# The first token half turned ahead at the end of a stage, in a two-layer transformer on one core

## The chip, the cores and the metric

The kernel runs on one core of one Trainium2 chip. The core has a matrix engine (PE), a vector engine (DVE), a scalar engine (ACT), GpSimd (POOL) and SyncE (SP), which only issues DMAs here, and 16 DMA engines that bring data from device memory into the on-chip memory. PE writes its results into banks of a separate accumulator memory (PSUM), from which DVE and ACT read them. Each engine has its own list of instructions and waits for the others by semaphores. The metric is the device time of one execution in microseconds (us).

## The reference

256 tokens of width 1024 go through seven parts, each of which adds its result to the residual `h`, with an RMS norm ahead of it. Cut to what matters:

```python
h = x
h = h + even_mixer(rms_norm(h, ln_mix[0]), ...)        # layer0_mix
h = h + swiglu(rms_norm(h, ln_ffn[0]), ...)            # f0, width 2816
h = h + gated_deltanet(rms_norm(h, ln_mix[1]), ...)    # gdn
h = h + moe_swiglu(rms_norm(h, ln_ffn[1]), ...)        # 8 experts, 2 per token, width 3584
...
def rmsnorm(x, w):
    xf = x.astype(jnp.float32)
    y = xf * lax.rsqrt(jnp.mean(xf * xf, axis=-1, keepdims=True) + EPS)
    return (y * w.astype(jnp.float32)).astype(x.dtype)
...
def swiglu_2(x, w_gu, w_down):
    g, u = jnp.split(x @ w_gu, 2, axis=-1)
    return (jax.nn.silu(g) * u) @ w_down
```

The second block follows on the same tokens: a feed-forward part (f1, width 2816), a token mixing with three branches (mixing) and another feed-forward part (f2, width 2816). Its parts have a second norm behind them (`f1post`, `mixpost`, `f2post`), ahead of the sum with the residual. Everything is fp32.

## The kernel before

**Precision and weights.** Each fp32 operand is split into a high part and the rest, and a product is three matmuls: high x high, high x low of either side (`mm3`, L274). The weights come as units of 1 MB. `Stream._load` (L204) issues a unit's DMA into a `raw` buffer, `_piece` (L221) lets ACT copy its half into `hi` (L229) and DVE subtract to `lo` (L230). There are two `raw` buffers for the whole program, and a feed-forward stage adds six of its own from the stage's memory pool. That memory was the stage's before, so the first DMA into one of them waits until the last reader of what lay there is done.

**Tokens.** The 256 tokens are two halves, t = 0 and t = 1, of 128 rows: `h[t]`. At the end of a stage each half gets its sum, and at four places `norm(t)` (L438) follows at once: ACT squares both 512-wide parts with a row sum, DVE forms `rs`, POOL raises it to -0.5, DVE writes `xn` (L269) in two instructions. After f1 and mixing `post_add` (L1253) stands ahead of it, the second norm with the same pattern (`pj`, `prs`). The next stage begins with `norm_T` (L425). It calls `norm_turn(0)` (L454), which lets PE transpose the half in two groups of four 128x128 blocks (L280), each into a PSUM bank; then ACT copies a bank into the high part of `x` and DVE subtracts to its low part (L292). The turn of the second half is kept as `turn_late` and called some way into the stage.

**The feed-forward stages.** `ffn` (L567) goes over 11 blocks f of 256 columns. For each and each half, 24 matmuls of gate and up go into a bank `gu`; ACT and DVE make `hv` from it; PE transposes it (`tr`), it is split into `hh` and `hl`, and 12 matmuls add to the two banks `y`. At the last block `done(t)` is called as soon as the half's `y` is complete. layer0_mix and mixing end with `out_proj`, whose matmuls write banks `mm`.

**What sets the order.** The code says which operation needs which; when the program is built, a list scheduler places the operations in one list per engine, with its own estimate of their times. On the chip each engine takes its list in order. Names in a row are those of tiles: `gu<-hi,x` is a gate and up matmul with weights `hi` that writes bank `gu`. In layer0_mix and the experts the banks of `norm_turn` are called `gu` before, in gdn and mixing `sd`, after the function that the next stage hands in.

Of the kernel before, what the change touches and what calls it, by code (L numbers as in the profile page):

```python
# [181 lines left out]
class Stream:  # L182
    def __init__(self, nc, rawp, hip, units, ends):
        self.nc, self.hip, self.units, self.ends = nc, hip, units, list(ends)
        self.pools = {0: [rawp, NRAW, []], 1: [None, 0, []]}
        self.raw, self.hi, self.lo = {}, {}, {}
        self.i = self.nl = self.np = 0
        self.limit = self.stop = 0
# [58 lines left out]
class Kernel:  # L247
    def __init__(self, ctx, tc, a, out):
        self.ctx, self.tc, self.nc, self.a, self.out = ctx, tc, tc.nc, a, out
        self.sides = []  # L250
        self.nev = 0
        self.moe_es = None
        self.normed = {}


    def act(self, out, in_, func, **kw):
# [167 lines left out]
    def norm_T(self, ps, late=False):  # L424

        for t in range(2):
            if t not in self.normed:
                self.norm(t)
        self.norm_turn(0, ps)
        self.turn_late = lambda: self.norm_turn(1, ps)  # L430
        if not late:
            self.turn_late()
        if self.gains:
            self.rowload(self.gain, self.gains.pop(0))
        self.W.open()

    def norm(self, t):

        h = self.h[t]
        ss = self.st.tile([128, 2], F32, name="ss", tag="ss")  # L440
        rs = self.st.tile([128, 1], F32, name="rs", tag="rs")
        xn = self.xn("xn")
        for n in range(2):
            s = slice(n * 512, n * 512 + 512)
            self.act(xn[:, s], h[:, s], AF.Square, scale=1.0 / 32, accum_out=ss[:, n:n + 1])
        self.ts(rs, ss[:, 0:1], ss[:, 1:2], EPS, ADD, ADD)
        self.last_pow = self.nc.gpsimd.tensor_tensor(rs, rs, self.mhalf[:, 0:1], ALU.pow)  # L447
        for n in range(2):
            s = slice(n * 512, n * 512 + 512)
            self.last_xn = self.stt(xn[:, s], h[:, s], rs, self.gain[:, s], MUL, MUL)  # L450
        self.normed[t] = xn

    def norm_turn(self, t, ps):
        xn, tok = self.normed.pop(t), slice(t * 128, t * 128 + 128)  # L454
        for n in range(2):
            p = ps()
            for c in range(4):
                self.tr(p[:, c * 128:c * 128 + 128], xn[:, n * 512 + c * 128:n * 512 + c * 128 + 128])
            self.split(self.xh[:, 4 * n:4 * n + 4, tok], self.xl[:, 4 * n:4 * n + 4, tok],
                       p.rearrange("p (c t) -> p c t", c=4))  # L460
# [193 lines left out]
    def layer0_mix(self):  # L654
        nc, tc, W = self.nc, self.tc, self.W
        with ExitStack() as es:
            pool = es.enter_context(tc.tile_pool(name="l0", bufs=1))
            sd, ps = self.banks("sd", "a"), self.banks("mm", "b")
# [208 lines left out]
            def add(t, n, p):  # L867
                s = slice(n * 512, n * 512 + 512)
                self.tt(self.h[t][:, s], p, self.h[t][:, s], ADD)
                if n == 1 and self.gains:  # L870
                    self.norm(t)
            self.drive(self.out_proj((yh, yl), ps, add))


# [353 lines left out]
    def ffn_phase(self, name, nf, post=None, final=False):  # L1228
        nc, tc = self.nc, self.tc
        with ExitStack() as es:  # L1230
            pool = es.enter_context(tc.tile_pool(name=name, bufs=1))
            gu, tr, y4 = self.banks("gu", "a"), self.banks("tr", "a"), self.banks("y", "b")
            self.W.phase(pool, 6)
            self.pad(pool, 128)
            self.norm_T(gu, True)
            with self.after(self.last_pow):
                pw = None if post is None else self.rowload(pool.tile([128, 1024], F32, name="pw"), post)
            y = [[y4(), y4()] for _ in range(2)]

            def done(key, t, yt):  # L1240
                if pw is None:
                    for n in range(2):
                        s = slice(n * 512, n * 512 + 512)
                        self.tt(self.h[t][:, s], yt[n], self.h[t][:, s], ADD)
                else:
                    self.post_add(t, yt, pw, 0.5, final)
                if not final:
                    self.norm(t)
            seq = [((self.xh, self.xl), 0, f == 0, f == nf - 1) for f in range(nf)]
            self.drive(self.ffn(seq, 2, pool, gu, tr, lambda key: y, done, first=self.turn_late))  # L1250

# [24 lines left out]
    def moe(self):  # L1276
# [4 lines left out]
        with ExitStack() as es:  # L1281
# [123 lines left out]
            def scatter(e, yh, yl):  # L1405
                for t in range(2):
                    for n in range(2):
                        s = slice(n * 512, n * 512 + 512)
                        p = sc()
                        self.mm(p, ohT[e][:, t * 128:t * 128 + 128], yh[:, s], True, False)  # L1410
                        self.mm(p, ohT[e][:, t * 128:t * 128 + 128], yl[:, s], False, True)
                        self.stt(self.h[t][:, s], p, gate[:, t, e:e + 1], self.h[t][:, s], MUL, ADD)
                        yield
                    if e == 7 and self.gains:
                        self.norm(t)

            def done(e, t, yt):
                yh, yl = (self.xn(n, dt=F32R) for n in ("yh", "yl"))
                for n in range(2):
                    s = slice(n * 512, n * 512 + 512)  # L1420
                    self.split(yh[:, s], yl[:, s], yt[n])
                self.sides.append(scatter(e, yh, yl))
# [81 lines left out]
    def mixing(self):  # L1504
        nc, tc, W = self.nc, self.tc, self.W
        with ExitStack() as es:
            pool = es.enter_context(tc.tile_pool(name="mx", bufs=1))
            sd, ps = self.banks("sd", "a"), self.banks("mm", "b")
# [330 lines left out]
            def fin(t, n, p):  # L1839
                z[t].append(p)  # L1840
                if n == 1:
                    self.post_add(t, z[t], pw, 1.0)
                    self.norm(t)
            self.drive(self.out_proj(X, ps, fin, True))


# [81 lines left out]
```

## Time and profile before

| what | before |
| --- | --- |
| median of 3 runs | 2270.36 us (2268.29 to 2271.34) |
| profiled execution | 2270.24 us, span 2268.5 us |
| PE busy | 2203.4 us, 97% of the span |
| DVE busy | 1709.2 us, 75% |
| ACT busy | 1390.6 us, 61% |
| POOL busy | 194.6 us, 9% |
| moved by DMA | 561.65 MB, 248 GB/s on average |

A span is the time from the first to the last instruction of one profiled execution; the 1.7 us by which its own time is longer lie around it. The busy shares are means over seven stages. What an edit at a stage's end is worth is read from the rows of that place.

### The profile page before, as it was taken

What the parts mean: (1) busy time and instruction counts of PE and PEld (TensorE: products, weight loads), DVE (VectorE), ACT (ScalarE), POOL (GpSimd) and SP (SyncE); (2) the same over time, 40 slices, a digit from 0 to 9 for tenths busy, and PEclk for the clock granted to TensorE, in tenths of its full rate; (3) what the DMA queues carried; (4) which work ended last, traced back from release to release, by engine and by line L of the source; (5) the groups of instructions that cost most, each with busy time, mean ns of one, the idle gap of its engine ahead of it and who ended that gap; (6) DMA issues with size and microseconds to landing.
All of it is one profiled execution on the core that took longest, in us unless ns stands there. A gap on an engine that the chain in (4) does not pass through costs nothing.

```text
span 2268.5 us, 29759 instructions
## 1 busy us (share of the span) xinstructions
PE 2203.4 (97%) x11398; PEld 1818.9 (80%) x11398; DVE 1709.2 (75%) x2220; ACT 1390.6 (61%) x1978; POOL 194.6 (9%) x324
## 2 busy tenths in 40 slices
PE   7899999998998999999999999999999999999998
PEld 6788877886887888888888888887887888787886
DVE  7754558876997999999999999995546667676544
ACT  5844456545776777777777777774445446345442
POOL 2000003232000000000100000000000000000000
PEclk9999999999999999999999999999999999999999
DMA  7375433225997999989999999977533543456540
GB/s 266 128 293 182 149 108 112 76 96 230 365 375 298 339 362 376 359 352 358 378 359 348 369 363 375 356 293 296 187 129 133 202 167 117 167 202 271 200 149 19
DMA packets 79701, 561.65 MB, mean 248 GB/s; under 512 B 8912, under 2 KB 9296, under 8 KB 12992
## 3 DMA queue, kind: packets, MB, share of 16 engines
q1 hardware_dynamic: 52272, 373.57, 43.8%
q0 software_dynamic: 26992, 185.58, 21.8%
q8 instruction: 92, 1.51, 0.3%
q10 hardware_dynamic: 288, 0.52, 0.1%
q14 instruction: 57, 0.47, 0.1%
HBM read 557.54 MB, written 2.10 MB: 247 GB/s over the span
## 4 chain that ended last, share of the span: by engine, by line
PE 67%; DVE 1%; issue 0%; ACT 0%; POOL 0%; POOLq 0%; DVEq 0%
PE gu L272 34%; PE y L272 17%; PE mm L272 12%; PE sd L272 2%; PE tr L280 1%; PE sc L272 1%; PE sd L280 0%; DVE pj L269 0%; DVE lo L230 0%; DVE h L260 0%; DVE h L269 0%; DVE xn L269 0%; POOL rs L447 0%; ACT hi L229 0%; ACT pj L257 0%
## 5 line engine op out<-in xcount | busy, mean ns | idle before, releaser
L230 DVE TENSOR_TENSOR lo<-raw,hi 128x1024 fp32r<-128x1024 f32 x1040 | 1242.4, 1225 | 289.6 <-ACT hi L229 281.3
L229 ACT ACTIVATE hi<-raw 128x1024 fp32r<-128x1024 f32 x1040 | 1060.7, 1054 | 394.9 <-PE gu L272 151.8
L272 PE MATMUL gu<-hi,x 128*128 128x512 f32 x2400 | 793.5, 397 | 11.1 <-PEq L1439 6.5
L272 PEld LDWEIGHTS gu<-hi,x 128*128 128x128 f32 x2400 | 453.1, 189 | 105.8 <-issue 6.9
L272 PE MATMUL gu<-lo,x 128*128 128x512 f32 x1200 | 470.7, 392 | 0.0
L272 PE MATMUL y<-hi,hh 128*128 128x512 f32 x712 | 277.7, 390 | 1.0 <-ACT hh L257 0.9
L272 PE MATMUL y<-lo,hh 128*128 128x512 f32 x712 | 277.2, 389 | 0.0
L272 PE MATMUL y<-hi,hl 128*128 128x512 f32 x712 | 276.3, 389 | 0.0
L272 PEld LDWEIGHTS gu<-lo,x 128*128 128x128 f32 x1200 | 227.4, 189 | 44.1 <-DVE lo L230 0.2
L272 PE MATMUL mm<-x,hi 128*128 128x512 f32 x576 | 210.5, 406 | 1.1 <-ACT hi L229 1.1
L272 PE MATMUL mm<-hi,x 128*128 128x512 f32 (+1 forms) x640 | 203.8, 391 | 2.2 <-DVE x L292 1.3
L257 ACT ACTIVATE sg<-gu 128x256 f32<-128x256 f32 x178 | 68.3, 384 | 201.1 <-PE gu L272 200.5
L272 PE MATMUL mm<-x,lo 128*128 128x256 f32 x576 | 164.6, 286 | 0.7 <-DVE lo L230 0.7
L216 POOL DMA_DIRECT2D raw<-in_w_moe_dram x167 | 88.5, 530 | 886.9 <-DVE lo L230 765.7
L272 PEld LDWEIGHTS y<-hi,hh 128*128 128x128 f32 x712 | 133.7, 188 | 29.6 <-ACT hh L257 2.3
L272 PEld LDWEIGHTS y<-hi,hl 128*128 128x128 f32 x712 | 133.6, 188 | 28.8 <-DVE hl L292 1.0
L272 PEld LDWEIGHTS y<-lo,hh 128*128 128x128 f32 x712 | 133.7, 188 | 27.4
L272 PEld LDWEIGHTS mm<-hi,x 128*128 128x128 f32 x640 | 119.3, 189 | 27.6 <-DVE x L292 2.5
L260 DVE TENSOR_TENSOR hv<-sg,gu 128x256 f32<-128x256 f32 x178 | 74.1, 416 | 74.2 <-ACT sg L257 74.2
L272 PEld LDWEIGHTS mm<-x,hi 128*128 128x128 f32 x576 | 109.1, 190 | 25.3 <-ACT hi L229 1.4
L272 PE MATMUL mm<-lo,x 128*128 128x512 f32 (+1 forms) x320 | 123.9, 387 | 0.9 <-DVE lo L230 0.9
L272 PEld LDWEIGHTS mm<-x,lo 128*128 128x128 f32 x576 | 109.8, 191 | 2.2 <-DVE lo L230 1.2
(436 smaller groups left out, 2134.6 us busy)
## 6 DMA issues: line engine op xcount, KB each, us to landing
raw<-in_w_moe_dram SPq DMA_DIRECT2D x169, 1024.0 KB, 7.0
raw<-in_w_moe_dram POOLq DMA_DIRECT2D x167, 1024.0 KB, 7.2
raw<-in_w_f_dram SPq DMA_DIRECT2D x99, 1024.0 KB, 5.0
raw<-in_w_mix_dram SPq DMA_DIRECT2D x40, 1024.0 KB, 4.8
raw<-in_w_oin_dram SPq DMA_DIRECT2D x16, 1024.0 KB, 4.8
raw<-in_w_ein_dram SPq DMA_DIRECT2D x7, 1024.0 KB, 6.5
raw<-in_w_br_dram SPq DMA_DIRECT2D x6, 1024.0 KB, 4.7
raw<-in_w_memkv_dram SPq DMA_DIRECT2D x4, 1024.0 KB, 4.8
```

The lines of the kernel that those rows point to most:

```text
L216: (self.nc.gpsimd if self.turns and u % 2 and u < self.limit else self.nc.sync).dma_start(r, self.units[u])
L229: self.nc.scalar.activation(hi[:, s], r[:, s], AF.Copy)
L230: self.nc.vector.tensor_tensor(self.lo[u][:, s], r[:, s], hi.bitcast(F32)[:, s], SUB)
L257: return self.nc.scalar.activation(out, in_, func, **kw)
L260: self.nc.vector.tensor_tensor(out, a, b, op)
L272: self.nc.tensor.matmul(out, lhsT, rhs, start=start, stop=stop, skip_group_check=True)
L280: self.nc.tensor.transpose(out, in_, self.C("ident") if ident is None else ident)
```

## The change

A new function `norm_ahead(t)` takes the place of `norm(t)` at the four places where a stage ends with its norm: layer0_mix, the feed-forward stages f0 and f1, the experts and mixing (five stage ends in all). It norms the half and, for the first half, turns and splits it right there, with banks named `nt` of the same ring of PSUM banks. A flag, `turned0`, tells the next stage's `norm_T` to skip what is done. The end of gdn is as before. The number of instructions on every engine is the same.

```diff
+        self.turned0 = False
...
         for t in range(2):
-            if t not in self.normed:
+            if t not in self.normed and not (t == 0 and self.turned0):
                 self.norm(t)
-        self.norm_turn(0, ps)
+        if not self.turned0:
+            self.norm_turn(0, ps)
+        self.turned0 = False
...
+    def norm_ahead(self, t):
+
+        self.norm(t)
+        if t == 0:
+            self.norm_turn(0, self.banks("nt", "a"))
+            self.turned0 = True
...
                 if n == 1 and self.gains:
-                    self.norm(t)
+                    self.norm_ahead(t)
...
                 if not final:
-                    self.norm(t)
+                    self.norm_ahead(t)
...
                     if e == 7 and self.gains:
-                        self.norm(t)
+                        self.norm_ahead(t)
...
                     self.post_add(t, z[t], pw, 1.0)
-                    self.norm(t)
+                    self.norm_ahead(t)
```

**The end of f1 on PE.** Before, the last 12 `y` matmuls of the first half are followed by the gate and up matmuls of the second half's last block:

```order
L272 MATMUL y<-lo,hh 128x512
L272 MATMUL y<-hi,hl 128x512
L272 MATMUL gu<-hi,x_71 128x512
L272 MATMUL gu<-lo,x_71 128x512
L272 MATMUL gu<-hi,x_71 128x512 x2
```

33 instructions later the first half is transposed (`sd`), between the `y` of the second half:

```order
L272 MATMUL y<-hi,hl 128x512
L280 MATMUL tr<-c_ident,hv 128x128 x2
L280 MATMUL sd<-c_ident,xn 128x128 x4
L272 MATMUL y<-hi,hh 128x512
L272 MATMUL y<-lo,hh 128x512
L272 MATMUL y<-hi,hh 128x512
```

Now the list has 24 `y` in a row, then all eight transposes, and only then the 24 gate and up matmuls:

```order
L273 MATMUL y<-lo,hh 128x512
L273 MATMUL y<-hi,hl 128x512
L281 MATMUL nt<-c_ident,xn 128x128 x8
L273 MATMUL gu<-hi,x_71 128x512
L273 MATMUL gu<-lo,x_71 128x512
L273 MATMUL gu<-hi,x_71 128x512 x2
L273 MATMUL gu<-lo,x_71 128x512
```

The transposes moved ahead of 24 `gu` matmuls and behind nine more `y`, in the list of the engine that waits for their input.

**The end of mixing on PE.** Before, the transposes follow the last matmul of the output projection (`mm`), and the f2 stage's `gu` follow them:

```order
L272 MATMUL mm<-lo,x_71 128x512
L272 MATMUL mm<-hi,x_71 128x512
L280 MATMUL gu<-c_ident,xn 128x128 x8
L272 MATMUL gu<-hi,x_71 128x512
L272 MATMUL gu<-lo,x_71 128x512
L272 MATMUL gu<-hi,x_71 128x512 x2
```

Now they stand ahead of the last 18 `mm`, with one `mm` between the two groups:

```order
L273 MATMUL mm<-hi,x_71 128x512 x2
L273 MATMUL mm<-lo,x_71 128x512
L281 MATMUL nt<-c_ident,xn 128x128 x4
L273 MATMUL mm<-hi,x_71 128x512
L281 MATMUL nt<-c_ident,xn 128x128 x4
L273 MATMUL mm<-hi,x_71 128x512
```

The `gu` follow the last `mm` directly, and after 24 or 25 of them come two transposes of the second half; the other six stand 11 matmuls further on:

```order
L273 MATMUL gu<-lo,x_71 128x512
L273 MATMUL gu<-hi,x_71 128x512 x2
L281 MATMUL gu<-c_ident,xn 128x128 x2
L273 MATMUL gu<-lo,x_71 128x512
L273 MATMUL gu<-hi,x_71 128x512 x2
L273 MATMUL gu<-lo,x_71 128x512
```

What moved is eight transposes ahead of 18 matmuls, and six of the second half behind some `gu`.

**The end of layer0_mix on PE.** Before, the transposes follow the last `mm` of the output projection, as in mixing:

```order
L272 MATMUL mm<-lo,yh 128x512
L272 MATMUL mm<-hi,yl 128x512
L280 MATMUL gu<-c_ident,xn 128x128 x8
L272 MATMUL gu<-hi,x_71 128x512
L272 MATMUL gu<-lo,x_71 128x512
```

Now they stand ahead of the last 12, in two groups with one matmul between:

```order
L273 MATMUL mm<-lo,yh 128x512
L273 MATMUL mm<-hi,yl 128x512
L281 MATMUL nt<-c_ident,xn 128x128 x4
L273 MATMUL mm<-hi,yh 128x512
L281 MATMUL nt<-c_ident,xn 128x128 x4
L273 MATMUL mm<-lo,yh 128x512
```

What moved is the eight transposes, ahead of 12 matmuls. At the end of f0 the list changes as at f1 (24 `y`, eight `nt`, 24 `gu`); at the end of the experts PE's list is the same but for the banks' names, and on DVE the two subtractions of the first half's `x` stand ahead of the second half's last `xn` instruction instead of behind it.

## Rows read from the trace of the kernel before

**Rows 1.** The page: busy us (share of the span) and instructions of each engine.

```profile
PE 2203.4 (97%) x11398; PEld 1818.9 (80%) x11398; DVE 1709.2 (75%) x2220; ACT 1390.6 (61%) x1978; POOL 194.6 (9%) x324
```

**Rows 2.** PE timeline, end of f1: start us, us, instruction, [idle before <-releaser].

```profile
1724.16 0.39 PE L272 MATMUL y<-hi,hl 128*128 128x512 f32 x1
1724.38 0.39 PE L272 MATMUL gu<-hi,x 128*128 128x512 f32 x1
...
1732.77 0.63 PE L280 MATMUL sd<-c_ident,xn 128*128 128x128 f32 x4 [0.52 <-DVE xn L269]
...
1747.02 0.50 PE L272 MATMUL mm<-lo,x 128*128 128x512 f32 x1 [0.63 <-DVE lo L230]
```

**Rows 3.** DVE timeline, end of f1.

```profile
1726.20 1.41 DVE L269 SCALAR_TENSOR_TENSOR pj<-y,prs,pw 128x512 f32<-128x512 f32 x2 [0.68 <-POOL prs L1261]
...
1728.73 2.36 DVE L230 TENSOR_TENSOR lo<-raw,hi 128x1024 fp32r<-128x1024 f32 x2
...
1731.87 1.42 DVE L269 SCALAR_TENSOR_TENSOR xn<-h,rs,gain 128x512 f32<-128x512 f32 x2 [0.33 <-POOL rs L447]
```

**Rows 4.** PE timeline, end of mixing and start of f2.

```profile
2065.67 1.04 PE L280 MATMUL gu<-c_ident,xn 128*128 128x128 f32 x8
2067.10 0.50 PE L272 MATMUL gu<-hi,x 128*128 128x512 f32 x1 [0.39 <-ACT x L257]
...
2070.80 0.79 PE L272 MATMUL gu<-hi,x 128*128 128x512 f32 x1 [2.97 <-DVE x L292]
```

**Rows 5.** Stretches: us, busy time of each engine, PE's granted clock (PEclk), DMA.

```profile
374.50:377.00 2.50, 2.50 (x16) 2.28 (x17) 1.52 (x4) 2.50 (x6) 2.17 (x4) 1.00 0.00 0
689.50:695.00 5.50, 5.48 (x14) 4.23 (x15) 0.97 (x4) 0.00 (x0) 0.00 (x0) 0.50 0.45 183
1545.00:1551.00 6.00, 5.07 (x12) 3.48 (x13) 5.38 (x7) 4.12 (x5) 1.10 (x2) 0.50 1.01 409
2071.00:2074.00 3.00, 3.00 (x8) 2.32 (x9) 1.88 (x4) 0.00 (x0) 1.13 (x2) 0.50 1.01 426
```

**Rows 6.** PE timeline, three more pauses (gdn, experts, start of f1).

```profile
374.47 0.60 PE L272 MATMUL sd<-c_ident,cv 128*128 128x1 f32 x4 [2.09 <-ACT cv L257]
...
689.52 0.77 PE L272 MATMUL gu<-hi,x 128*128 128x512 f32 x1 [6.48 <-PEq L1439]
...
1543.52 0.63 PE L280 MATMUL gu<-c_ident,xn 128*128 128x128 f32 x4 [3.34 <-DVE xn L269]
```

**Rows 7.** DVE timeline, end of mixing.

```profile
2061.68 1.41 DVE L269 SCALAR_TENSOR_TENSOR xn<-h,rs,gain 128x512 f32<-128x512 f32 x2 [0.74 <-POOL rs L447]
...
2067.54 1.41 DVE L269 SCALAR_TENSOR_TENSOR pj<-mm,prs,pw 128x512 f32<-128x512 f32 x2 [0.73 <-POOL prs L1261]
```

**Rows 8.** DMA issues of SyncE, start of f0 and of f2.

```profile
133.68 0.33 SPq L216 DMA_DIRECT2D raw<-in_w_f_dram  x1
...
2069.08 0.33 SPq L216 DMA_DIRECT2D raw<-in_w_f_dram  x1
```

**Rows 9.** ACT timeline, start of f0 and of f2.

```profile
138.80 2.01 ACT L229 ACTIVATE hi<-raw 128x1024 fp32r<-128x1024 f32 x2 [3.03 <-DMA raw<-in_w_f_dram]
...
2074.17 1.06 ACT L229 ACTIVATE hi<-raw 128x1024 fp32r<-128x1024 f32 x1 [3.25 <-DMA raw<-in_w_f_dram]
```

**Rows 10.** DVE timeline, end of layer0_mix.

```profile
130.57 1.42 DVE L269 SCALAR_TENSOR_TENSOR xn<-h,rs,gain 128x512 f32<-128x512 f32 x2 [0.68 <-POOL rs L447]
```

**Rows 11.** PE timeline, end of layer0_mix.

```profile
133.44 1.03 PE L280 MATMUL gu<-c_ident,xn 128*128 128x128 f32 x8
```

**Rows 12.** DVE timeline, end of f0.

```profile
313.83 1.42 DVE L269 SCALAR_TENSOR_TENSOR xn<-h,rs,gain 128x512 f32<-128x512 f32 x2 [0.75 <-POOL rs L447]
```

**Rows 13.** PE timeline, end of f0 and start of gdn.

```profile
326.62 1.07 PE L280 MATMUL sd<-c_ident,xn 128*128 128x128 f32 x6 [0.36 <-DVE xn L269]
...
331.79 0.50 PE L272 MATMUL mm<-hi,x 128*128 128x512 f32 x1 [0.65 <-DVE x L292]
```

**Rows 14.** DVE timeline, end of the experts.

```profile
1546.15 1.28 DVE L292 TENSOR_TENSOR x<-gu,x 128x512 fp32r<-128x512 f32 x2
```

## The prediction

> **What bounds the kernel now.** I read the page first: the matrix engine (PE) is busy 97% of the span [rows 1], so an edit that only re-orders work can gain no more than PE's pauses around it, and loses what it adds to them. Then PE's timeline at the five places where a first token half will be turned earlier: the ends of layer0_mix, f0, the experts, f1 and mixing. The reader is to see in it the bracket, PE's idle time ahead of a row and who ended it. Then the engines that feed the turn (DVE, ACT), the DMA issues of SyncE, and PE's granted clock after long pauses.
>
> **What the change adds and removes.** No operation is added: both programs hold the same instructions on every engine. Eight transposes of the first half, with two ACT copies and two DVE subtractions, move in front of other work. PE takes its instructions in the program's order, at every place that I read, so everything behind the transposes waits until DVE has written the normed rows (`xn`). Each boundary is priced by walking the new order with the durations of before; matmuls start 0.23 us apart [rows 2].
>
> *End of f1.* Before, after the last `y` matmul of the first half (1724.16), PE had 21 `gu` and 12 `y` of the second half to do while the norm ran [rows 2]. The norm is long: DVE forms `pj` at 1726.20, two `lo` pieces stand ahead of its `rs`, and `xn` begins at 1731.87, its first half (0.71 of 1.42) done at 1732.6 [rows 3]. Before, PE waited 0.52 for it, and 0.63 later for a `lo` [rows 2]. Now nine `y` are left ahead of the transposes, 9 x 0.23 = 2.1 us, to about 1726.6; the 24 `gu` stand behind them. PE is idle from 1726.6 to 1732.6, 6.0 us, and 0.2 more for the second half of `xn`. What hid the norm, 24 x 0.23 = 5.5 us of `gu`, comes after it. All of that work still has to be done, so the loss is 6.0 + 0.2 + about 0.3 for the second half's `x` later on, less the waits of before that go, 0.52 + 0.63: 5.35. Walked on to the second half's `mm`, where both have the same work behind them, I get 1755.2 against 1750.1: +5.1, which I take, between 4.5 and 5.9. The weights that are late next (the unit behind the first two waits for their `lo`, and those `hi` now wait for the moved `gu`) arrive when PE gets there, by the walk.
>
> *PE's clock.* After a pause of 2.97 us at 2070.80 [rows 4] the granted clock is 0.50 for 3.0 us; after 3.34 it is 0.50 over six; after 6.48 over 5.5; after 2.09 it stays 1.00 [rows 5, 6]. 0.50 is 1.2 instead of 2.4 GHz, so such a stretch costs half its length: 1.5 to 3.1 us, middle 2.2. The new pause at the end of f1 should cost that: +2.2. The Trainium skill, "TensorE: Matmul & The Clock Gate", section "Why this matters for your kernels", speaks against this change here: it warns of pauses between bursts of matmuls, since the engine then falls back to its lower clock. This trace agrees in its three pauses of 2.97 us and more. By that rule the sum stands as it is; without it the two clock terms, 4.4 in all, would be nil.
>
> *End of mixing.* Here a pause goes: 0.39 + 2.97 us in which PE waits for `x`, whose DVE half stands behind three `lo`, `prs`, `pj` and `h` [rows 4, 7], and the 1.5 us of clock behind it. Now the transposes stand ahead of the last 18 matmuls of the projection. PE gets there at 2061.3 (19 x 0.23 before the old ones' 2065.67); `xn` begins at 2061.68 and its first half is done at 2062.4 [rows 7]: 1.1 us of waiting and eight transposes of 1.04 in all [rows 4] put the last matmul 2.05 later. `pj` of the second half waits for that matmul; and SyncE's loads of the f2 stage's own buffers wait for `pj`, because these buffers lie on memory of the mixing stage. The issue at 2069.08 [rows 8] slips to about 2071.2, and the first `hi` copy, which waited for that DMA until 2074.17 [rows 9], to 2076.2. PE, no longer held by `x`, runs its 24 `gu` from 2067.8 to 2073.3 and stands there until that `hi` is done, 2077.3: a pause of 4.0 in place of 3.36. At 2078.5 both have done 25 `gu`; before had turned all of the second half, after lacks six transposes: +0.9. The new pause brings its own slow clock, +2.2, where the walk of before had the old one in its times. Bounds: 0.7 and 4.
>
> *End of layer0_mix.* The same chain without a pause to remove. The transposes stand ahead of the last 12 matmuls; `xn` begins at 130.57 (first half done 131.3) [rows 10], PE would come to them at 130.7 (12 x 0.23 before 133.44, where the old ones began). So 0.6 + 0.2 of waiting and about 0.9 of transposes stand ahead of the last matmul, which releases the memory that SyncE's load waits for: issue 133.68 [rows 8] to 135.3, the `hi` that waited 3.03 us for it [rows 9] from 138.80 to 140.3. PE has 24 `gu` with their weights and then needs that unit. The transposes would otherwise have filled this gap [rows 11]. +1.5, between 0.9 and 1.7.
>
> *End of f0.* As at f1, with a shorter norm and no `pj`. 24 `y`, then the transposes: PE there at about 313.2, `xn` begun at 313.83 [rows 12], done by half at 314.5: 1.35 of waiting. Later the matmuls of the first half run out before the second half's `xn` (its `y` now come after the 24 `gu`, 4.7 us later): about 2.0 idle, then 0.8 and 0.3 for its `x`, whose ACT copies stand behind a table load. That is 4.4, less the 0.36 and 0.65 of before [rows 13]: 3.4; walked to an instruction that both have (331.79 before, 334.6 now) it is +2.8, which I take, between 1 and 4.5, since gdn's re-ordered helpers make this walk the least sure. No single pause is over 2.1 us, where the one at 374.47 shows no loss of clock [rows 5, 6].
>
> *End of the experts.* PE's order stays. On DVE the two `x` subtractions stand ahead of the second half's last `xn` piece instead of behind it; PE waits for them, and they began at 1546.15 [rows 14], so one `xn` piece of about 0.65 less: -0.6, between -0.65 and -0.3. The 3.34 us ahead of the transposes [rows 6] stay: the norm itself is late there.
>
> **Sum.** 5.1 + 2.2 + 0.9 + 2.2 + 1.5 + 2.8 - 0.6 = 14.1 us on the profiled execution's 2270.24, which is 0.12 below the median of the runs: 2284.3, about 0.6% slower. All lower bounds with no clock term give 4.5 + 0.7 + 0.9 + 1.0 - 0.65 = 6.5; all upper ones 5.9 + 3.1 + 4.0 + 1.7 + 4.5 - 0.3 = 18.9.
>
> **Rivals.**
> - *The clock doesn't fall in the two new pauses.* For it: a pause at 374.47 left no mark [rows 5, 6]. Against: the three longer ones did. 14.1 - 4.4 = 9.7: 2279.9.
> - *The f2 weights are not late.* If SyncE's loads at the end of mixing don't slip, PE gets back 0.39 + 2.97 + 1.5 = 4.9 there, in place of losing 3.1: 14.1 - 3.1 - 4.9 = 6.1: 2276.3; with the low bounds elsewhere (6.5 - 0.7 - 4.9 = 0.9) 2271, no change. For it: the pause that is removed is named as DVE's `x`, not as a DMA [rows 4]. Against: ACT waits 3.25 us for that very DMA [rows 9].
> - *Faster: the transposes find their rows written.* If PE came to them at the ends of layer0_mix, f0, f1 and mixing only after `xn`, nothing would be held, no `pj` would slip, and the pauses ahead of f2 and f1 would pay: -4.9 - 0.6 = -5.5: 2264.8. It decides at the end of f1: PE would have to come 6 us later than the walk says. `y` matmuls of 0.23 us can't make that; only a much shorter norm could, and its length is in [rows 3].
> - *The turn is not moved at all* is excluded by the order at four places; at the experts it nearly is so.
>
> **Chances.** Forecast 0.60 (its own range 2278 to 2290), no clock loss 0.14, weights not late 0.10, the same with low bounds 0.09, faster 0.07. A measurement of this kernel can tell about 0.2%, 4.5 us, from no change. The first three are slower: 0.84; same 0.09; faster 0.07. The range goes from 2274 to 2290: it leaves out the last two and a little above.
>
> **What the profile after would show.** Right: a bracket of about 6 us ahead of `nt` transposes at the end of f1, ended by DVE `xn`, and clock 0.50 behind it; a first `gu` of f2 without a bracket, then some 4 us of waiting on ACT `hi`, with SyncE's issue 2 us later against the stage's last matmul; the first `hi` of f0 1.5 us later; some 1.4 us ahead of `nt` at the end of f0. Wrong: if the `nt` rows have no bracket, the walk of PE's order is wrong; if f2 runs through, the DMA's tie to `pj` is; if the idle ahead of `nt` is there but the stage's end isn't later, other waits took it up, which the low idle of gdn and mixing speaks against.

## The result, and the profile after

The change makes the kernel slower: 2285.97 us, median of 4 runs (2285.65 to 2286.36), against 2270.31 for the kernel before (4 runs, 2268.29 to 2271.34). The ratio is 1.0067, interval 1.0054 to 1.0079. The profiled execution took 2286.22 us, its span is 2284.6, 16.1 more than before. PE is busy by little more than before [rows 1], on the page of the kernel after:

```profile
PE 2208.8 (97%) x11398; PEld 1822.9 (80%) x11398; DVE 1708.7 (75%) x2220; ACT 1391.6 (61%) x1978; POOL 194.3 (9%) x324
```

So 5.4 of the 16.1 us are PE busy for longer with the same instructions, as at a lower clock, and the other two thirds are idle time on PE. They are looked for at the places where the turn was moved.

**End of f1.** PE's timeline after the change (start us, us, instruction, idle before and who ended it), beside [rows 2]:

```profile
1738.44 1.94 PE L281 MATMUL nt<-c_ident,xn 128*128 128x128 f32 x8 [6.18 <-DVE xn L270]
1740.03 0.77 PE L273 MATMUL gu<-hi,x 128*128 128x512 f32 x1
...
1759.40 0.50 PE L273 MATMUL mm<-lo,x 128*128 128x512 f32 x1 [0.30 <-DVE lo L230]
```

PE stands idle for 6.18 us ahead of the eight transposes of the first half, until DVE has written `xn`, where before there was a wait of 0.52. The transposes then take 1.94 us, against 1.29 for eight at the start of f1 below: the clock is down. The stretches of the kernel after (us, busy time per engine, then PEclk, DMA share, GB/s) show it, beside [rows 5]:

```profile
1732.20:1738.40 6.20, 0.06 (x1) 0.00 (x0) 5.54 (x9) 3.23 (x6) 0.55 (x1) 0.89 0.10 18
1738.50:1743.00 4.50, 4.50 (x15) 3.92 (x16) 1.84 (x3) 1.19 (x2) 0.00 (x0) 0.50 0.50 208
1743.00:1748.00 5.00, 5.00 (x21) 4.06 (x21) 2.07 (x2) 2.43 (x4) 0.00 (x0) 0.92 0.00 0
...
2091.00:2095.00 4.00, 3.90 (x9) 2.79 (x10) 3.46 (x3) 2.96 (x4) 0.00 (x0) 0.50 1.01 423
337.00:341.00 4.00, 3.97 (x12) 2.73 (x13) 2.43 (x5) 1.16 (x2) 0.59 (x1) 0.57 0.64 162
1553.00:1556.00 3.00, 2.58 (x6) 1.82 (x6) 2.46 (x5) 1.57 (x2) 1.06 (x2) 0.50 1.02 423
1556.00:1562.00 6.00, 6.00 (x27) 4.89 (x26) 4.66 (x5) 2.83 (x4) 0.00 (x0) 0.99 0.93 372
```

The first three rows: the pause, PEclk 0.50 behind it, and the return. The other rows are those of the end of mixing, f0 and the experts, to which the next paragraphs come.

**End of mixing.** PE again, beside [rows 4]:

```profile
2075.75 0.63 PE L281 MATMUL nt<-c_ident,xn 128*128 128x128 f32 x4 [1.05 <-DVE xn L270]
...
2091.06 0.79 PE L273 MATMUL gu<-hi,x 128*128 128x512 f32 x1 [4.46 <-ACT hi L229]
```

The `gu` of f2 need no longer wait for `x`; the pauses of 0.39 and 2.97 are gone. In their place PE waits 1.05 ahead of the transposes, and 4.46 for the third weight unit's `hi`. SyncE's issues and ACT's first copies of such a unit, of f0 and f2, beside [rows 8, 9]:

```profile
136.60 3.09 SPq L216 DMA_DIRECT2D raw<-in_w_f_dram  x6
...
2084.40 0.33 SPq L216 DMA_DIRECT2D raw<-in_w_f_dram  x1
```

```profile
141.47 2.01 ACT L229 ACTIVATE hi<-raw 128x1024 fp32r<-128x1024 f32 x2 [3.47 <-DMA raw<-in_w_f_dram]
...
2089.95 2.00 ACT L229 ACTIVATE hi<-raw 128x1024 fp32r<-128x1024 f32 x2 [1.60 <-DMA raw<-in_w_f_dram]
```

The `hi` of f2 waits for its DMA, issued at 2084.40, as it did before for the one issued at 2069.08. Counted from the end of the matmul that now stands just ahead of the transposes (2074.70, before 2061.53), the issue is 2.15 later: 9.70 against 7.55. The pause of 4.46 ends in a stretch at PEclk 0.50 too (the row 2091.00 above).

**End of layer0_mix.** PE, beside [rows 11]:

```profile
132.69 0.63 PE L281 MATMUL nt<-c_ident,xn 128*128 128x128 f32 x4 [0.60 <-DVE xn L270]
...
142.59 0.50 PE L273 MATMUL gu<-hi,x 128*128 128x512 f32 x1 [0.63 <-ACT hi L229]
...
147.44 0.50 PE L273 MATMUL gu<-lo,x 128*128 128x512 f32 x1 [0.56 <-DVE lo L230]
```

0.60 ahead of the transposes, and then two waits for the units in f0's own buffers, 0.63 for the first one's `hi` and 0.56 for the next one's `lo`, that were not there.

**End of f0.** PE, DVE and POOL, beside [rows 12, 13]:

```profile
317.42 1.29 PE L281 MATMUL nt<-c_ident,xn 128*128 128x128 f32 x8 [1.34 <-DVE xn L270]
...
336.30 1.29 PE L281 MATMUL sd<-c_ident,xn 128*128 128x128 f32 x8 [3.67 <-DVE xn L270]
```

```profile
333.79 3.03 DVE L270 SCALAR_TENSOR_TENSOR xn<-h,rs,gain 128x512 f32<-128x512 f32 x2 [0.73 <-POOL rs L450]
```

```profile
333.20 0.55 POOL L450 TENSOR_TENSOR rs<-rs,mhalf 128x1 f32<-128x1 f32 x1 [2.78 <-DVE rs L267]
...
334.32 1.27 POOL L1196 TENSOR_TENSOR sgate<-sgate,rows 128x512 f32<-128x512 f32 x1
```

The first wait is 1.34. The second is 3.67, and the two `xn` instructions that end it take 3.03 us in place of 1.42. While they run, POOL multiplies gdn's gate (`sgate`) with norm weights. Before, that product came 5 us behind `xn`:

```profile
325.72 1.42 DVE L269 SCALAR_TENSOR_TENSOR xn<-h,rs,gain 128x512 f32<-128x512 f32 x2 [0.73 <-POOL rs L447]
...
332.25 1.29 POOL L1186 TENSOR_TENSOR sgate<-sgate,rows 128x512 f32<-128x512 f32 x1 [4.29 <-ACT sgate L257]
```

**End of the experts.** DVE and PE, beside [rows 14]:

```profile
1552.37 0.75 DVE L270 SCALAR_TENSOR_TENSOR xn<-h,rs,gain 128x512 f32<-128x512 f32 x1 [0.66 <-POOL rs L450]
1553.04 1.28 DVE L293 TENSOR_TENSOR x<-nt,x 128x512 fp32r<-128x512 f32 x2
1554.23 0.74 DVE L270 SCALAR_TENSOR_TENSOR xn<-h,rs,gain 128x512 f32<-128x512 f32 x1
```

```profile
1551.06 1.29 PE L281 MATMUL nt<-c_ident,xn 128*128 128x128 f32 x8 [3.34 <-DVE xn L270]
...
1553.77 0.80 PE L273 MATMUL gu<-hi,x 128*128 128x512 f32 x1 [0.42 <-DVE x L293]
```

The first half's `x` now comes between the two last `xn`. PE's pause of 3.34 stays. The second pause, ahead of the third `gu`, is 0.42 here. In the trace of before, and in that of the run below with only layer0_mix changed, which leaves this place as it was, that `gu` reads:

```profile
1546.89 0.79 PE L272 MATMUL gu<-hi,x 128*128 128x512 f32 x1 [0.93 <-DVE x L292]
...
1549.24 0.80 PE L273 MATMUL gu<-hi,x 128*128 128x512 f32 x1 [0.38 <-DVE x L293]
```

The pause alone doesn't size the gain: 0.38 stands behind transposes that took 1.94 us at the lower clock, 0.93 behind transposes of 1.29. From the first transpose to this `gu` it is 3.37 us in both (1543.52 and 1545.87 to these rows), and 2.71 after the change (1551.06 to 1553.77): 0.66 less. The stretch at PEclk 0.50 is about 3 us here (1553 to 1556 in the stretches above) where it was six in the trace of before [rows 5]; it is about 3 us as well in three traces that leave the place as it was.

**By place.** To size each, I take from PE's timeline the time between two instructions that stand on either side of the place in both programs: the matmul that stands just ahead of the transposes after the change (its end) to the first `tr` of the next stage at layer0_mix and mixing; the last pair of `tr` of the stage's first half to the first matmul of the next stage's second kind (`mm<-x,hi`) at f0 and f1; the last `sc` (its end) to the first `tr` of f1 at the experts. "Alone" is the difference in the run in which only that place is changed, from the experiments below. "Place not changed" is the range of the same time over the ten traces (at mixing eight) of before and of the experiments that leave the place as it was.

| end of | forecast | before, after, us | difference | alone | place not changed | ratio alone |
| --- | --- | --- | --- | --- | --- | --- |
| layer0_mix | +1.5 | 24.7, 26.1 | +1.4 | +1.5 | 24.4 to 24.7 | 1.0007 (0.9998 to 1.0016) |
| f0 | +2.8 | 29.4, 34.8 | +5.4 | +5.8 | 29.2 to 29.4 | 1.0021 (1.0012 to 1.0030) |
| experts | -0.6 | 28.6, 26.7 | -1.9 | -1.4 | 26.3 to 28.7 | 0.9988 (0.9979 to 0.9997) |
| f1 | +7.3 | 40.2, 48.1 | +7.9 | +7.3 | 40.2 | 1.0027 (1.0018 to 1.0037) |
| mixing | +3.1 | 30.4, 33.2 | +2.9 | +2.4 | 30.4 to 31.7 | 1.0005 (0.9996 to 1.0014) |
| sum | +14.1 | | +15.7 | +15.6 | | 1.0048 |

The five differences give 15.7 of the 16.1 us of the spans. At the experts and at mixing, a difference of two traces says little: there a place that nobody changed moves by 2.4 and 1.3 us, with the length and position of the stretch at the lower clock. Against the medians of the places not changed (24.4, 29.3, 27.5, 40.2 and 31.4), the kernel after differs by +1.7, +5.5, -0.8, +7.9 and +1.8.

### The profile page after: what moved, and what is told of

Read it like the earlier page. It is cut to its first block, busy times and chain, and to the rows that moved or that the text cites. A ratio compares the mean times of both kernels' runs of the same rounds, so it can differ in the third digit from the quotient of the medians.

```text
span 2284.6 us, 29764 instructions
## 1 busy us (share of the span) xinstructions
PE 2208.8 (97%) x11398; PEld 1822.9 (80%) x11398; DVE 1708.7 (75%) x2220; ACT 1391.6 (61%) x1978; POOL 194.3 (9%) x324
## 4 chain that ended last, share of the span: by engine, by line
PE 67%; DVE 1%; ACT 0%; issue 0%; DMA 0%; POOL 0%; POOLq 0%; DVEq 0%; SPq 0%; ACTq 0%
PE gu L273 34%; PE y L273 17%; PE mm L273 12%; PE sd L273 2%; PE tr L281 1%; PE sc L273 1%; PE sd L281 0%; DVE pj L270 0%; DMA raw<-in_w_f_dram 0%; DVE lo L230 0%; PE nt L281 0%; DVE h L261 0%; DVE h L270 0%; ACT hi L229 0%; POOL prs L1271 0%
## 5 line engine op out<-in xcount | busy, mean ns | idle before, releaser
L273 PE MATMUL gu<-hi,x 128*128 128x512 f32 x2400 | 793.7, 397 | 11.5 <-PEq L1449 6.0
L273 PEld LDWEIGHTS mm<-hi,x 128*128 128x128 f32 x640 | 120.1, 190 | 27.5 <-ACT x L258 2.0
```

What stands on the lines that cost most here:

```text
L273: self.nc.tensor.matmul(out, lhsT, rhs, start=start, stop=stop, skip_group_check=True)
```

## The experiments

The theory: each place costs by itself what PE stands ahead of transposes that come too early, with the clock's fall behind a long pause, and at two places with a DMA that hangs on the stage's last matmuls. Its rivals: that the other order behind the places costs or gives back time, that the clock is not a cause, and that the weights are late anyhow. Runs of the kernel before on the same chips had medians of 2270.4 to 2270.6.

**One place at a time.** Four runs, each with `norm_ahead` at one of the places and `norm` at the others, as here for f1:

```diff
-                    self.norm_ahead(t)
+                    (self.norm_ahead if name == "f1" else self.norm)(t)
```

> The first half is turned ahead only at the end of layer0_mix. My theory (each place costs by itself what PE waits there) takes its size from the two traces: an instruction of f0 came 2.65 us later after the change than before, so about +2.65 us, 2273.0. The rival theory, that the loss is not made at the places but by the different order of everything behind them, expects less than +1 here, since behind layer0_mix the order is the same.

Measured: 2272.12 us, ratio 1.0007 (0.9998 to 1.0016). The place itself is 1.5 longer with the waits of 0.6, 0.7 and 0.6. The offset of 2.65 between the two traces, which I gave as the expectation, had a stretch at the lower clock ahead of this place in it, which the trace before doesn't have at that spot; the place is worth 1.5 against the trace of before and 1.8 against the nine others that leave it as it was (24.4). The interval of the ratio takes in the rival's "less than +1" too; it is the place that speaks for the theory.

> Only at the end of f0. My theory: two waits ahead of the transposes, 1.3 us for the first half and 3 to 4 us for the second, and then a stretch at the lower clock: +5.1 us by the offset of the two traces (7.75 at the start of the experts less 2.65), 2275.4. The rival, that gdn's other order costs or gives back time on its own: the waits are there, but the start of the experts is moved by something else than +5, between +1 and +8.

Measured: 2275.24, ratio 1.0021 (1.0012 to 1.0030); the same pauses of 1.35 and 3.67, the place 5.8 longer, as the theory expects. The start of the experts, which was to tell the theory from its rival, is 8.0 us later, counted from the same `tr` (390.1 against 382.0). But the rest of gdn has 27.4 us at the lower clock in that trace and 11.5 in the one of before, so whether gdn's other order costs or gives back time stays open.

> Only at the end of the experts. PE's list is that of before; two subtractions come 0.65 us earlier on DVE. Both traces together show 1.9 us less here, 1.3 of it by a shorter stretch at the lower clock. If that belongs to the change: 2268.5, a second pause of 0.4 in place of 0.93 and some 3 us at half clock. The rival: the shorter slow stretch was chance, and the gain is 0.5: 2269.8.

Measured: 2267.41, ratio 0.9988 (0.9979 to 0.9997). Of the five places alone, the only one whose ratio lies below 1. In its trace the stretch at the lower clock is as long as before, so the shorter one doesn't belong to the change; the third `gu` starts 2.79 us behind the first transpose, 0.58 less than without the change. So the place gives the rival's 0.5, or a little more; the -1.4 of the whole place lies inside what it does unchanged. By the interval of the ratio the whole run gains 0.7 to 4.8 us; where more than 0.6 would come from, the traces don't show.

> Only at the end of f1. My theory: 6.2 us of idle PE ahead of the transposes, then a stretch of about 4 us at the lower clock: +7.6 us (the offset of the two traces at the end of mixing less that in f1), 2277.9; the largest part of the whole. The rival, that the waits and the clock of the full change act on each other, expects a sum of the five places alone that is not that of the full change, and here less than 6.

Measured: 2276.37, ratio 1.0027 (1.0018 to 1.0037), the pause 6.18 and the place 7.3 longer, as expected. By times the five ratios alone add up to 1.0048, which is 10.9 us against 15.2 for all at once; each has an interval of 0.0009 to either side, 0.002 or more for the sum, so this is no contradiction, and no proof that they add up. By the traces, where a place is measured without what chance does elsewhere, they do: 15.6 and 15.7, with the chance at the experts and mixing that the table shows.

**Mixing, and what its weights hang on.** First mixing alone, then the same with the line that gives a feed-forward stage six `raw` buffers of its own changed for f2, and that line alone in the kernel before:

```diff
-            self.W.phase(pool, 6)
+            self.W.phase(pool, 0 if final else 6)
```

> Only at the end of mixing. My theory: PE no longer waits for the first half's x (2.97 + 0.39 us of before go), but the transposes hold the last matmuls, the second norm's pj is late by 2, the DMA of f2's first own buffer with it, and PE stands some 4.5 us for its hi: +2.8 us, 2273.1. The rival, that the wait removed is a gain: -3 to -5, 2266.

Measured: 2271.60, ratio 1.0005 (0.9996 to 1.0014), the place 2.4 longer than in the trace of before (1.1 to 2.4 by the range in the table). PE's waits from the end of mixing into f2 in that run (engine, who waits for whom: us in total, times, longest):

```profile
PE gu L273 <- ACT hi L229: 4.0, 1, 4.0
PE nt L281 <- DVE xn L270: 1.0, 1, 1.0
PE gu L273 <- DVE lo L230: 0.5, 1, 0.5
```

> As the one before, but f2 has no raw buffers of its own (0 in place of 6), so its weights go through the two that the whole program shares, whose release hangs on lo and not on pj. My theory (the removed wait was replaced by the weights, which hang on memory of mixing): the 4.5 us of waiting for hi go, x is there, the transposes' own wait of 1 us stays: 3 to 5 us faster than with only mixing changed, 2268 to 2269 or less, and no pause of over 2 us at the start of f2. The rival, that PE waits at that place whatever comes (DMA time, x): still about 2273.

Measured: 2266.80, ratio 0.9978 (0.9968 to 0.9988). The same view:

```profile
PE nt L281 <- DVE xn L270: 1.1, 1, 1.1
PE gu L273 <- DVE lo L230: 0.2, 1, 0.2
```

The wait for `hi` is gone, the one for `xn` stays, the place is 27.1 us, 3.3 shorter than before, and the clock doesn't fall in it. So with weights that don't hang on mixing's memory, the removed wait is a gain, with the slow stretch behind it; with weights that do, it was replaced.

> The kernel before, with no own raw buffers in f2. It shows whether that alone changes the time. My theory: PE's wait there is for x, whose subtraction stands behind lo, prs, pj and h; the weights come earlier, but PE still stands for x: within 2 us of 2270.3. The rival, that two buffers are too few for f2: slower by more than 3, through waits for DMA all through f2, which would also spoil the run before this one.

Measured: 2269.33, ratio 0.9992 (0.9983 to 1.0001). PE there:

```profile
2065.87 0.50 PE L272 MATMUL gu<-hi,x 128*128 128x512 f32 x1 [0.39 <-ACT x L257]
...
2068.81 0.50 PE L272 MATMUL gu<-hi,x 128*128 128x512 f32 x1 [2.21 <-ACT hi L229]
2069.57 0.79 PE L272 MATMUL gu<-hi,x 128*128 128x512 f32 x1 [0.25 <-DVE x L292]
```

The pause is split, 2.21 of it now put down to ACT `hi`; the three sum to 2.85 in place of 3.36, and the place is 30.2 us. Two buffers are enough for f2, and they alone change nothing that can be told: the gain of the run before takes both edits.

**The clock behind the pause.** At f1, `norm_turn` first transposes a block of the residual 20 times into the bank that it then overwrites:

```diff
             p = ps()
+            if n == 0:
+                for c in range(fill):
+                    self.tr(p[:, c % 4 * 128:c % 4 * 128 + 128], self.h[t][:, 512:640])
```

> Only at the end of f1, and 20 more transposes, of the residual and into the bank that the turn then overwrites, ahead of the turn's own: work that is thrown away, put into the pause. They can start some 4 us before xn is there and last 2.6 us, so the pause falls into two of about 2 and 1 us while the transposes of xn start when they did. If the clock's fall is caused by the length of the pause: PEclk stays near 1.00 behind it and the time is 1.5 to 2.5 us below that with only f1 changed, 2275.5 to 2276.5. The rival (the clock falls for another reason, or is not what costs): 2277.9 as without them, or more.

Measured: 2275.51, ratio 1.0020 (1.0011 to 1.0029), against 1.0027 with f1 alone: the two intervals overlap, so the times don't settle it. PE's timeline and two stretches in the trace do more:

```profile
1725.31 3.82 PE L281 MATMUL nt<-c_ident,h 128*128 128x128 f32 x20 [2.37 <-DVE h L261]
1729.03 1.38 PE L281 MATMUL nt<-c_ident,xn 128*128 128x128 f32 x8
1730.17 0.48 PE L273 MATMUL gu<-hi,x 128*128 128x512 f32 x1
```

```profile
1725.50:1729.00 3.50, 3.50 (x20) 3.23 (x18) 2.84 (x5) 0.71 (x4) 0.55 (x1) 0.58 0.06 9
1729.00:1734.00 5.00, 5.00 (x26) 4.18 (x26) 1.93 (x3) 1.91 (x3) 0.00 (x0) 0.95 0.51 206
```

The clock fell all the same, already behind the pause of 2.37, so the filling took 3.82 us where I had reckoned 2.6. But it had risen again when the `gu` came, and the transposes of `xn` start as far behind the first half's `tr` as without the filling (12.0 us, 12.1 there): the place is 45.8 us, 1.7 shorter than with f1 alone (47.5), and still 5.6 longer than before, with more work in it. So about 1.7 of the 7.3 belong to the lower clock and some 5.6 to the order. That a shorter pause leaves the clock up, as I expected, did not hold here; so whether the length of the pause is what brings it down stays open.

**f0: why the second wait was longer than forecast.** The product of the gate on DVE in place of POOL, with only f0 changed:

```diff
-                    nc.gpsimd.tensor_tensor(sg, sg, outn.unsqueeze(1).to_broadcast([128, 4, 128]), MUL)
+                    nc.vector.tensor_tensor(sg, sg, outn.unsqueeze(1).to_broadcast([128, 4, 128]), MUL)
```

> Only at the end of f0, as in the second run, and the product of gdn's gate with its norm weights on DVE instead of POOL (the same arithmetic). In that second run the two xn instructions of the second half took 3.03 us in place of 1.42 while POOL worked on that product beside them. If the one slows the other, xn takes 1.4 again and PE's pause of 3.67 ahead of the second half's transposes falls to about 2.1, and with it a slow stretch of the clock may go; 1.6 to 3.3 us less than with f0 alone: 2272 to 2273.7. The rival, that xn is slow there for another reason (the DMAs, the clock): it stays at 3.0, the pause at 3.7 or more, 2275.

Measured: 2275.13, ratio 1.0024 (1.0015 to 1.0033), no less than f0 alone. DVE and PE at the place:

```profile
335.01 1.41 DVE L270 SCALAR_TENSOR_TENSOR xn<-h,rs,gain 128x512 f32<-128x512 f32 x2 [0.73 <-POOL rs L450]
336.34 1.22 DVE L230 TENSOR_TENSOR lo<-raw,hi 128x1024 fp32r<-128x1024 f32 x1
```

```profile
335.90 1.29 PE L281 MATMUL sd<-c_ident,xn 128*128 128x128 f32 x8 [2.05 <-DVE xn L270]
...
339.09 0.73 PE L273 MATMUL mm<-hi,x 128*128 128x512 f32 x2 [1.02 <-DVE x L293]
```

`xn` takes 1.41 again and the pause is 2.05, so POOL's product was what slowed it. The place is 32.8 us, 2.5 shorter than in the run with f0 alone, though the product, now on DVE ahead of the second `x`, makes a new wait of 1.02. The clock doesn't fall in it, where it was at 0.50 for some 7 us in the other trace, so part of the 2.5 is the clock's. That the whole time is not shorter doesn't contradict this: DVE has the product four times in gdn, and the rest of gdn is 1.1 longer here than with f0 alone (355.9 and 354.8 us, both with 27.4 at the lower clock). What is left, 1.4 us or 0.0006, is less than the intervals of the two ratios can tell.

**layer0_mix without buffers of its own.** The change there alone, and `0 if name == "f0" else 6` in the line on the buffers.

> Only at the end of layer0_mix, and f0 has no raw buffers of its own, so that its weights don't wait for the last matmul of the stage before. My theory (there the transposes cost through the DMA that they delay): PE's waits of 0.66 for hi and 0.56 for lo, some 6 and 11 us into f0, go; the 0.6 ahead of the transposes stays. From the last matmul ahead of the transposes to the first turn of f0's own values it takes 24.7 us before, 26.2 with the change there; now about 25.1. The rival (the transposes cost what they wait and last, and the weights come late anyhow): 26 again.

Measured: 2270.74, ratio 1.0000 (0.9991 to 1.0009). PE's waits from the transposes to the first turn of f0, first with layer0_mix alone, then here:

```profile
PE gu L273 <- ACT hi L229: 0.7, 1, 0.7
PE nt L281 <- DVE xn L270: 0.6, 1, 0.6
PE gu L273 <- DVE lo L230: 0.6, 1, 0.6
```

```profile
PE nt L281 <- DVE xn L270: 0.6, 1, 0.6
```

Both waits for weights are gone, and the place is 24.2 us, against 26.2 and, before, 24.7 (24.4 in the nine other traces that leave it as it was). So nothing is left of the loss; the ratio agrees, but its interval alone would not tell this from the run with layer0_mix alone.

**The experts and mixing together.**

> The first half is turned ahead at the two places where a pause went, the end of the experts and the end of mixing, and f2 has no raw buffers of its own. By the parts: -3.4 us at the end of mixing, -0.5 to -1.9 at the experts' end: 2265 to 2266.5, faster than before. A rival, that the two do not add up because the clock's slow stretches come and go by chance: 2267 to 2268.

Measured: 2266.28 us, ratio 0.9982 (0.9973 to 0.9991): 0.18% faster than the kernel before, and so some 0.8% faster than the changed one (0.9982 / 1.0067). The place at mixing is 3.4 shorter than before. The one at the experts is 1.9 shorter (26.7), which unchanged traces reach too; the third `gu` is 0.66 earlier, as after the full change. Against mixing and its buffers alone (2266.80, 0.9978) the experts add nothing that can be told.

## Why the prediction was right

*PE in order, and a norm that is not there yet.* The pauses ahead of the transposes were forecast as 6.0, 1.35, 1.1 and 0.6 us and are 6.18, 1.34, 1.05 and 0.60. They follow from three things that the rows of before have: when `xn` is written, how many matmuls the new order leaves ahead of the transposes, and their 0.23 us.

*End of f1.* +5.1 and +2.2 for the clock: measured 7.9, alone 7.3. The run with the filling divides the 7.3 into 5.6 for the order and 1.7 for the clock.

*End of mixing.* +0.9 and +2.2: measured 2.9, alone 2.4, and less against the other traces that leave the place as it was (1.8 and 1.3 against their median): that it comes so near 3.1 is partly the trace of before, whose slow stretch here was a short one. The walk of the DMA was right: the issue slips by 2.15 where 2.05 was forecast. The sign named for it, an issue 2 us later "against the stage's last matmul", was put wrongly: it is 3.25 us behind the end of that matmul before and after, since the last matmul is late with it. Shown by the buffers: the gain of some 3.3 us that the removed wait brings appears as soon as the weights no longer hang on `pj`. The rival "the f2 weights are not late" gave 4.9 for that case; it is refuted by the 4.46 that PE waits for `hi`.

*End of layer0_mix.* +1.5: measured 1.4, alone 1.5 (1.7 and 1.8 against the other traces). The issue of the DMA slips by 1.7, forecast 1.6. Without the DMA's tie the place is no longer than in any trace that leaves it as it was, in spite of the 0.6 that PE stands ahead of the transposes. PE's idle time there is 0.60 in all, against 0.25; why its instructions take that much less was not traced.

*End of f0.* The step that failed is a term that was too small: "about 2.0 idle" ahead of the second half's transposes, and "no single pause is over 2.1 us", so no clock term. It was 3.67, with a stretch at PEclk 0.57 behind it. The walk took `xn` at 1.42 us from [rows 12]; the new order of POOL set the gate's product beside it, and it took 3.03. With the product elsewhere the pause is 2.05 and the clock stays at 1.00 in that trace, which is the forecast. +5.4 in place of +2.8.

*End of the experts.* -0.6: measured 0.66, 0.66 and 0.58 less up to the third `gu`, in the three traces with the change; the ten without it have 3.37 or 3.38 there. What the whole place differs by, -1.9 and alone -1.4, is this and how the slow stretch lies over the pause and the first `gu`, which differs between executions.

*The clock.* That it falls behind the new pauses was right, at f1 and at f2; the size, 2.2 each, was taken from the lengths of single stretches (half of [rows 5] is 1.5 to 3.0), and the filling gave 1.7 at f1. That 2.09 us leaves no mark was read from one execution and does not hold in others (below). The rival without a fall of the clock is refuted by the rows at 0.50, that of a faster kernel by the 6.18.

The sum was 14.1 with 15.7 by the places. f0 is 2.6 too small, f1 0.6; against this stands the experts' 1.3, most of it chance. That the sum comes this near, with f0 at half its size, is partly luck.

## What to carry to other kernels

Work that is issued earlier on an engine that takes its instructions in order is only earlier if its input is there; otherwise everything behind it waits, and the work that used to cover the wait comes after it. Before moving such a step forward, count what is left between it and the producer's end at the engine's own spacing, and look for loads whose memory is released by the work that is pushed back. Where a wait is to be removed at a stage's start, free what the next stage's first loads hang on as well: either edit alone brought nothing at the end of mixing, both together brought 0.2%.

## What the runs showed of the hardware

*A short pause can be followed by the lower clock.* In the trace of before PE's pause of 2.09 in gdn left PEclk at 1.00 [rows 5, 6]. In the run with only the experts changed the same pause was 2.11 and the stretch behind it reads:

```profile
373.00:380.00 7.00, 6.78 (x35) 5.75 (x35) 3.96 (x13) 5.01 (x10) 2.80 (x6) 0.51 0.00 0
```

PEclk 0.51 over 7 us. The pause of 2.37 ahead of the filling was followed by a low clock too. Ten of the thirteen traces have this pause in gdn, with 2.06 to 2.11 us. In four of them the clock stays at 1.00, and PE's next 100 matmuls and transposes take 9.9 us; in the six others it is at 0.50 within 2 us, and they take 10.4 (two traces) or 11.9 us (four). So the same place costs nothing in one execution and 0.5 or 2.0 us in another. The end of mixing is another such case: PEclk 0.50 for 3 us in the trace of before [rows 5], and about twice as long in the traces of six of the runs above in which nothing was changed there. Such differences are likely a part of the spread of single runs, 2265 to 2275 us for the kernel before; how large a part was not measured.

*DVE and POOL side by side.* Two `xn` instructions on DVE (a scalar and two tensors, 128x512, fp32) took 3.03 us while POOL ran a 128x512 product of 1.27 us, and 1.41 without it: 1.6 us lost to 1.3 us of POOL's work. All of it is in the first of the two, which began 0.53 us ahead of the product and took 2.37 us in place of 0.75; the second took 0.74. The Trainium skill, "SBUF — State Buffer", section "Who interferes with whom", says that a DVE instruction with two inputs in that memory contends with a GpSimd instruction that reads there, and calls the ports that they share an exclusive lock. These rows agree: `xn` has two such inputs, `h` and `gain`, and lost a little more than the product lasts. That an engine with 9% of the span on it can lengthen the path in this way was not in my walk.
